# Queuing x sums and weight sums of the first seven-product unit behind the norm's last piece, in each MLP of a two-layer decoder step

## Chip, cores and metric

One core of a Trainium2 chip runs the whole program in one launch. The metric is the device time of one execution in microseconds (us). Engines are named as in the profile: PE is TensorE, DVE is VectorE, ACT is ScalarE, POOL is GpSimd, and SP issues the DMAs.

## What is computed

A step of a two-layer decoder for 512 prompt tokens and 8 x 4 sample tokens, 544 columns in all, with a model width of 1024. Layer 0 mixes tokens with sparse softmax attention, layer 1 with retention; each mixer is followed by an MLP of hidden width 4096. The change lies in the two MLPs:

```python
def _rms(xf):
    return xf * lax.rsqrt(jnp.mean(xf * xf, axis=-1, keepdims=True) + EPS)

def sqrelu_mlp(h, w1, w2):
    return jnp.square(jax.nn.relu(h @ w1)) @ w2
...
        yp = yp + sqrelu_mlp(rms_norm(yp, ln_mlp[i]), mlp_w_in[i], mlp_w_out[i])
        ys = ys + sqrelu_mlp(rms_norm(ys, ln_mlp[i]), mlp_w_in[i], mlp_w_out[i])
```

## The kernel before

**Tiling.** The activations stand transposed in eight tiles `xT[0..7]` of 128 features x 544 tokens; the profile and the queue listings call them x_112 to x_119. Matmuls are done in 32-bit parts: an operand is rounded by ACT (`h`) and DVE takes the rest (`l`), and three products h·h, h·l, l·h go to PE. `split_w` does this for a weight tile (ACT L465 writes `wh`, DVE L466 writes `wl`, two buffers of each), `split_into` for anything else (L662, L663). A 128-column output tile with eight k steps is 48 matmuls of 272 columns, done by `tile_of` (L506) into one of two `mm` PSUM buffers.

**The norm.** The mean square is not applied to x before the matmul but to its result. `take_pair` makes the operands of an x tile as soon as the mixer's output has been added to it (L656), and `square_x` squares it on ACT (L408). The squares of tiles 0 to 5 are added up on POOL, those of tiles 6 and 7 go to PE as they are. `row_rsqrt` sums over the features with small matmuls (L341), and twelve short DVE instructions (L344, then `rsqrt`, L323 to L328) make the root. `spread_rows` spreads it with four small matmuls (L351) and writes `RB`, one half by ACT (L353), one by DVE (L354). Results of a matmul are multiplied by RB as they leave PSUM.

**An MLP.** The first 512 hidden columns are done in four plain tiles, called tile 0 to 3 below. Tile 0 is done before RB exists, so ACT copies it out (`early`, L514); tiles 1 and 2 stay in the two `mm` buffers until DVE takes them with RB (`ev_first`, L1216), and tile 3 needs one of these buffers. ACT then squares (L1209), and `split_into` makes the hidden operands `hs`. The first down unit (two tiles of 24 matmuls, for x_112 and x_113) needs the hidden operands of all four tiles; the next one begins with x_114.

All later hidden columns use seven products in place of eight (`fast_block`, L570 for its matmuls). Such a unit of 256 columns needs sums of its weights: its `split` makes four sums (`add`, L546) and seven splits (`part`, L662 and L663). It also needs sums of x tiles, which `combine` makes once per MLP: two scaled copies on ACT (L444), four DVE instructions (L446, L447, L449, L450) and two splits for each of the four pairs of x tiles. The first such unit, F1 below, stands after the first two down units, the second, F2, two down units later. One product of F1 (`pa`, 12 matmuls) needs no sum of x tiles and only one split.

**What sets the order.** `run` walks over the units; `prepare` asks for loads and splits up to 9 us ahead, and `tick` advances the generators of `combine`. That is only the order of the program: a scheduler then places each instruction on its engine's queue by its own estimate of when it is ready, and allots the buffers. On the chip each queue runs in order, and an instruction whose data is not there holds all behind it. SP's queue waits before a load until a `raw` buffer (four) is free. `late_load` asks for one `raw` tile that nothing writes, before the load of F1.

Of the kernel before, what the change touches and what calls it, by code (L numbers as in the profile page):

```python
# [26 lines left out]
FT = mybir.dt.float32  # L27
# [117 lines left out]
def decoder_step(ctx, tc, x_prompt, x_sample, cache_k, cache_v, cache_kidx, state_ret, page_table,  # L145
# [73 lines left out]


# [98 lines left out]

    def rsqrt(x, w):  # L320

        y, a = w
        V.tensor_scalar(y.bitcast(I32), x.bitcast(I32), 1, None, op0=OP.logical_shift_right)  # L323
        V.tensor_scalar(y.bitcast(I32), y.bitcast(I32), -1.0, 1597463007.0, op0=OP.mult, op1=OP.add)
        for _ in range(3):
            V.tensor_tensor(a, y, y, op=OP.mult)
            V.scalar_tensor_tensor(a, a, -0.5, x, op0=OP.mult, op1=OP.mult)
            V.scalar_tensor_tensor(y, a, 1.5, y, op0=OP.add, op1=OP.mult)  # L328
        return y
# [75 lines left out]
    def square_x(k, n=KT - 2):  # L405

        sq = tmp.tile([128, T], FT, name="sq")
        A.activation(sq, xT[k], AF.Square)  # L408
        if k >= n:
            late.append(sq)  # L410
        elif k == 0:
            G.tensor_copy(acc[:, :T], sq)  # L412
        else:
            G.tensor_tensor(acc[:, :T], sq, acc[:, :T], op=OP.add)

# [3 lines left out]
    def take_pair(k, gi):  # L419
# [17 lines left out]
        square_x(k)  # L437

    def combine(i, gi):

        lo, hi = slice(0, HALF), slice(HALF, T)
        x0, x1 = hs_tile(FT), hs_tile(FT)
        for k, x in ((2 * i, x0), (2 * i + 1, x1)):
            A.activation(x, xT[k], AF.Identity, scale=gains[:, gi * 8 + k:gi * 8 + k + 1])  # L444
        n, t = hs_tile(FT), hs_tile(FT)
        V.tensor_tensor(t[:, lo], x1[:, hi], x0[:, hi], op=OP.subtract)  # L446
        V.tensor_tensor(n[:, lo], x0[:, lo], x0[:, hi], op=OP.subtract)  # L447
# [72 lines left out]
    def fast_block(src, c0, evac):  # L520
# [14 lines left out]
        def split():  # L535
# [3 lines left out]

            def part(name, a):  # L540
                W[name] = [fp.tile([128, 4, 128], FR, name=n, tag=n, bufs=b) for n, b in (("sh", 6), ("sl", 5))]
                split_into(*W[name], a)

            def add(a, b):
                t = fp.tile([128, 4, 128], FT, name="ss", tag="ss", bufs=3)
                V.tensor_tensor(t, a, b, op=OP.add)  # L546
# [655 lines left out]
    def mlp(l, done):  # L1202
        with ExitStack() as st:
# [15 lines left out]
            def up(c):  # L1219
# [9 lines left out]
                return fast_block(mlp_w_in[l], 512 * c, ev) + fast_block(mlp_w_in[l], 512 * c + 256, ev)  # L1229
# [8 lines left out]
            def late_load(load):  # L1238

                skipped = []  # L1240

                def once():
                    if not skipped:
                        skipped.append(raw_tile())
                    return load()
                return once

# [3 lines left out]
            for c in range(n):  # L1251
                down = dense4(mlp_w_out[l], 4 * c, lambda c=c: H[c], add_to_x(done if c == n - 1 else None))
                nxt = up(c + 1) if c + 1 < n else []
                if c == 0:
                    nxt[0].update(before=combined, load=late_load(nxt[0]["load"]))
# [348 lines left out]
```

## Time and profile before

| what | value |
|---|---|
| three runs | 1584.3, 1580.71, 1584.08 us; median 1584.08 |
| profiled execution | 1581.1 us, of which the span from first to last instruction is 1579.2 |
| mean granted TensorE clock | 0.992 of 2.4 GHz |
| DVE, ACT busy | 67% and 39% of the span |
| first MLP, second MLP begin | about 288 and 1190 us |

The span is cut by the profile into rows of one instruction, or of some that follow each other. A row gives its start and its duration. Rows that follow without a gap overlap a little, so the time that an instruction costs its queue is the distance from its start to the next one's start. A bracket at a row's end gives the time for which the engine had nothing to run before it, and what it is taken to have waited for.

### The profile page before, as it was taken

What the parts mean: (1) busy time and instruction counts of PE and PEld (TensorE: products, weight loads), DVE (VectorE), ACT (ScalarE), POOL (GpSimd) and SP (SyncE); (2) the same over time, 40 slices, a digit from 0 to 9 for tenths busy, and PEclk for the clock granted to TensorE, in tenths of its full rate; (3) what the DMA queues carried; (4) which work ended last, traced back from release to release, by engine and by line L of the source; (5) the groups of instructions that cost most, each with busy time, mean ns of one, the idle gap of its engine ahead of it and who ended that gap; (6) DMA issues with size and microseconds to landing.
All of it is one profiled execution on the core that took longest, in us unless ns stands there. A gap on an engine that the chain in (4) does not pass through costs nothing.

```text
span 1579.2 us, 28176 instructions
## 1 busy us (share of the span) xinstructions
PE 1527.9 (97%) x11670; PEld 1440.2 (91%) x11670; DVE 1059.9 (67%) x1950; ACT 611.9 (39%) x1036; POOL 190.5 (12%) x172
## 2 busy tenths in 40 slices
PE   7989899999999999999999999999998999999998
PEld 6689559899999999999899999999988999999998
DVE  6599774778677676556566465565568687677653
ACT  4423663545444444423232232223236454444432
POOL 3220320100000000212221122121210000000000
PEclk9999999999999999999999999999999999999999
DMA  6533252222332233223724622722812322332211
GB/s 177 156 98 94 71 185 81 81 81 81 107 107 86 82 101 107 79 79 109 246 67 163 197 84 91 260 71 73 274 60 64 105 83 82 107 107 82 83 51 57
DMA packets 135774, 172.53 MB, mean 109 GB/s; under 512 B 11660, under 2 KB 92630, under 8 KB 135646
## 3 DMA queue, kind: packets, MB, share of 16 engines
q1 hardware_dynamic: 135578, 170.72, 33.3%
q8 instruction: 91, 1.49, 0.4%
q14 instruction: 37, 0.30, 0.1%
q10 hardware_dynamic: 68, 0.02, 0.0%
HBM read 148.34 MB, written 25.01 MB: 110 GB/s over the span
## 4 chain that ended last, share of the span: by engine, by line
PE 87%; DVE 8%; DMA 2%; ACT 2%; issue 1%; SPq 0%; DVEq 0%; ACTq 0%
PE mm L506 56%; PE mm L570 16%; PE pa L570 2%; PE pb L1487 2%; PE pb L1513 1%; PE pa L1431 1%; DMA raw<-in_mlp_w_in_dram 1%; PE pa L1457 1%; DVE wl L466 1%; PE pb L1468 1%; PE pa L1041 1%; DVE sc L781 1%; PE pa L1014 1%; DVE m L780 1%; PE pb L1100 1%
## 5 line engine op out<-in xcount | busy, mean ns | idle before, releaser
L506 PE MATMUL mm<-xs,wh 128*128 128x272 f32 (+1 forms) x2784 | 501.4, 295 | 13.5 <-ACT r L1209 5.9
L506 PEld LDWEIGHTS mm<-xs,wh 128*128 128x128 f32 (+1 forms) x2784 | 410.0, 190 | 27.5 <-issue 8.9
L506 PE MATMUL mm<-hs,wh 128*128 128x272 f32 x2304 | 393.4, 289 | 3.2 <-DVE x L656 2.0
L506 PEld LDWEIGHTS mm<-hs,wh 128*128 128x128 f32 x2304 | 329.6, 189 | 5.5 <-DVE x L656 2.6
L465 ACT ACTIVATE wh<-raw 128x1024 fp32r<-128x1024 f32 x159 | 167.9, 1057 | 382.0 <-PE mm L506 356.9
L506 PE MATMUL mm<-xs,wl 128*128 128x272 f32 (+1 forms) x1392 | 297.5, 292 | 0.0
L570 PE MATMUL mm<-xs,sh 128*128 128x272 f32 x1344 | 259.1, 289 | 3.1 <-ACT r L583 1.8
L506 PE MATMUL mm<-hs,wl 128*128 128x272 f32 x1152 | 241.1, 288 | 0.0
L656 DVE TENSOR_TENSOR x<-mm,x 128x544 f32<-128x544 f32 x176 | 127.0, 723 | 163.4 <-PE mm L506 162.1
L506 PEld LDWEIGHTS mm<-xs,wl 128*128 128x128 f32 (+1 forms) x1392 | 222.7, 190 | 3.0 <-issue 1.1
L570 PEld LDWEIGHTS mm<-xs,sh 128*128 128x128 f32 x1344 | 210.3, 188 | 5.8 <-ACT r L586 3.5
L466 DVE TENSOR_TENSOR wl<-raw,wh 128x1024 fp32r<-128x1024 f32 x151 | 188.7, 1250 | 16.9 <-ACT wh L465 9.3
L570 PE MATMUL mm<-xs,sl 128*128 128x272 f32 x672 | 192.8, 287 | 0.0
L506 PEld LDWEIGHTS mm<-hs,wl 128*128 128x128 f32 x1152 | 182.1, 188 | 0.2
L570 PEld LDWEIGHTS mm<-xs,sl 128*128 128x128 f32 x672 | 126.3, 188 | 0.0
L662 ACT ACTIVATE sh<-ss 128x512 fp32r<-128x512 f32 x112 | 70.6, 630 | 123.8 <-PE mm L570 118.7
L663 DVE TENSOR_TENSOR sl<-ss,sh 128x512 fp32r<-128x512 f32 x112 | 76.7, 686 | 16.2 <-PE mm L570 16.2
L662 ACT ACTIVATE sh<-raw 128x512 fp32r<-128x512 f32 x84 | 53.1, 632 | 88.2 <-PE mm L570 70.8
L663 DVE TENSOR_TENSOR sl<-raw,sh 128x512 fp32r<-128x512 f32 x84 | 58.6, 698 | 9.3 <-PE mm L570 9.3
L1470 DVE SCALAR_TENSOR_TENSOR raw<-raw,pb 128x512 f32<-128x512 f32 x64 | 43.3, 684 | 24.9 <-PE pb L1468 15.8
L663 DVE TENSOR_TENSOR hs<-r,hs 128x544 fp32r<-128x544 f32 x64 | 46.1, 720 | 16.0 <-ACT hs L662 15.8
L412 POOL COPY acc<-sq 128x544 f32<-128x544 f32 x4 | 3.1, 780 | 444.8 <-ACT sq L408 444.8
(345 smaller groups left out, 1814.6 us busy)
## 6 DMA issues: line engine op xcount, KB each, us to landing
raw<-in_mlp_w_in_dram SPq DMA_DIRECT2D x32, 1024.0 KB
raw<-in_mlp_w_out_dram SPq DMA_DIRECT2D x32, 1024.0 KB
raw<-in_ret_w_in_dram SPq DMA_DIRECT2D x24, 1024.0 KB
raw<-in_state_ret_dram SPq DMA_DIRECT2D x32, 512.0 KB
out_dram<-raw SPq DMA_DIRECT2D x32, 512.0 KB
raw<-in_ret_w_out_dram SPq DMA_DIRECT2D x8, 1024.0 KB
raw<-in_att_w_in_dram SPq DMA_DIRECT2D x7, 1024.0 KB
raw<-in_cache_k_dram SPq DMA_DIRECT2D x32, 128.0 KB
```

Source lines behind the costliest of these rows:

```text
L465: A.activation(h, view, AF.Copy)
L466: eng.tensor_tensor(l, view, h.bitcast(FT), op=OP.subtract)
L506: PE.matmul(ps[:m, c, :HALF], w[:, k, m * t:m * (t + 1)], x[c] if isinstance(x, tuple) else x[:, HALF * c:HALF * (c + 1)], start=(k == 0 a ...
L570: PE.matmul(ps, a[:, i, :], b, start=(first and i == 0 and j == 0), stop=(i == 3 and j == 2), skip_group_check=True)
L656: V.tensor_tensor(two(xT[m]), halves(ps), two(xT[m]), op=OP.add)
L662: A.activation(dst_h, src, AF.Copy)
L663: V.tensor_tensor(dst_l, src, dst_h.bitcast(FT), op=OP.subtract)
L780: V.max(out=m8, in_=sc)
L781: V.match_replace(out=sc, in_to_replace=m8, in_values=sc, imm_value=TAKEN)
L1014: PE.matmul(ps[:, :W], qT[h][:, 128 * blk:128 * (blk + 1)], kT[h // 4][:, :W], start=True, stop=True)
L1470: V.scalar_tensor_tensor(sl, sl, gam4[h], pu, op0=OP.mult, op1=OP.add)
L1487: PE.matmul(ps[:, SP - WJ[j]:], v[:, j, 128 * e:128 * (e + 1)], a[:, AM[j]:AM[j] + WJ[j]], start=(j == 0 and v is vh and a is am[0]), stop ...
```

## The change

`behind(marks)` gives each instruction that is made inside it an order behind the marked instructions on the same engine; no semaphore is added. The marks are `last_in["N"]`, the last DVE instruction of the latest `rsqrt`, and `last_in["A"]`, the latest `square_x` on ACT. Behind them go: in each `combine`, the two scaled copies and the first two differences; and for F1 alone (`first`), all sums and splits of its weights. `late_load` is dropped. No instruction is added or taken away.

```diff
@@ -217,6 +217,14 @@
             for c in calls[1:]:
                 c()
 
+    @contextmanager
+    def behind(marks):
+
+        with ExitStack() as st:
+            for m in marks:
+                st.enter_context(tc.issue_after(m.ins))
+            yield
+
 
     follow, side, held = [], [], []
     norm = {"pending": False}
@@ -317,6 +325,8 @@
         return cr[:rows, lo:hi] if hi <= NCR else ca[:rows, lo - NCR:hi - NCR]
 
 
+    last_in = {}
+
     def rsqrt(x, w):
 
         y, a = w
@@ -325,7 +335,7 @@
         for _ in range(3):
             V.tensor_tensor(a, y, y, op=OP.mult)
             V.scalar_tensor_tensor(a, a, -0.5, x, op0=OP.mult, op1=OP.mult)
-            V.scalar_tensor_tensor(y, a, 1.5, y, op0=OP.add, op1=OP.mult)
+            last_in["N"] = V.scalar_tensor_tensor(y, a, 1.5, y, op0=OP.add, op1=OP.mult)
         return y
 
     def rsqrt_columns(x, n):
@@ -405,13 +415,14 @@
     def square_x(k, n=KT - 2):
 
         sq = tmp.tile([128, T], FT, name="sq")
-        A.activation(sq, xT[k], AF.Square)
+        ins = A.activation(sq, xT[k], AF.Square)
         if k >= n:
             late.append(sq)
         elif k == 0:
             G.tensor_copy(acc[:, :T], sq)
         else:
             G.tensor_tensor(acc[:, :T], sq, acc[:, :T], op=OP.add)
+        return ins
 
     XC = [{} for _ in range(KT // 2)]
     XP = [None] * KT
@@ -434,17 +445,19 @@
             h, l = XP[k] = xs_tile(), xs_tile()
             split(h, l, xT[k])
             XC[k // 2].update(b21=(h[:, lo], l[:, lo]), b22=(h[:, hi], l[:, hi]))
-        square_x(k)
+        last_in["A"] = square_x(k)
 
     def combine(i, gi):
 
         lo, hi = slice(0, HALF), slice(HALF, T)
-        x0, x1 = hs_tile(FT), hs_tile(FT)
-        for k, x in ((2 * i, x0), (2 * i + 1, x1)):
-            A.activation(x, xT[k], AF.Identity, scale=gains[:, gi * 8 + k:gi * 8 + k + 1])
-        n, t = hs_tile(FT), hs_tile(FT)
-        V.tensor_tensor(t[:, lo], x1[:, hi], x0[:, hi], op=OP.subtract)
-        V.tensor_tensor(n[:, lo], x0[:, lo], x0[:, hi], op=OP.subtract)
+        marks = list(last_in.values())
+        with behind(marks):
+            x0, x1 = hs_tile(FT), hs_tile(FT)
+            for k, x in ((2 * i, x0), (2 * i + 1, x1)):
+                A.activation(x, xT[k], AF.Identity, scale=gains[:, gi * 8 + k:gi * 8 + k + 1])
+            n, t = hs_tile(FT), hs_tile(FT)
+            V.tensor_tensor(t[:, lo], x1[:, hi], x0[:, hi], op=OP.subtract)
+            V.tensor_tensor(n[:, lo], x0[:, lo], x0[:, hi], op=OP.subtract)
         yield 0.9
         V.scalar_tensor_tensor(n[:, hi], n[:, lo], -1.0, x1[:, hi], op0=OP.mult, op1=OP.subtract)
         V.scalar_tensor_tensor(t[:, hi], n[:, hi], -1.0, x1[:, lo], op0=OP.mult, op1=OP.subtract)
@@ -517,7 +530,7 @@
                     release()
                 yield 1.5
 
-    def fast_block(src, c0, evac):
+    def fast_block(src, c0, evac, first=False):
 
 
 
@@ -537,13 +550,17 @@
             v = view().rearrange("p (i j) (f c) -> p i j f c", j=2, f=2)
             a11, a21, a12, a22 = (v[:, :, j, f, :] for j in range(2) for f in range(2))
 
+            marks = list(last_in.values()) if first else ()
+
             def part(name, a):
                 W[name] = [fp.tile([128, 4, 128], FR, name=n, tag=n, bufs=b) for n, b in (("sh", 6), ("sl", 5))]
-                split_into(*W[name], a)
+                with behind(marks):
+                    split_into(*W[name], a)
 
             def add(a, b):
                 t = fp.tile([128, 4, 128], FT, name="ss", tag="ss", bufs=3)
-                V.tensor_tensor(t, a, b, op=OP.add)
+                with behind(marks):
+                    V.tensor_tensor(t, a, b, op=OP.add)
                 return t
             part("a11", a11)
             yield 1.5
@@ -1226,7 +1243,8 @@
                     else:
                         V.scalar_tensor_tensor(r, r, 0.0, RB, op0=OP.max, op1=OP.mult)
                     hidden(c, r)
-                return fast_block(mlp_w_in[l], 512 * c, ev) + fast_block(mlp_w_in[l], 512 * c + 256, ev)
+                return fast_block(mlp_w_in[l], 512 * c, ev, c == 1) + \
+                    fast_block(mlp_w_in[l], 512 * c + 256, ev)
 
             n = DFF // 512
             H[0] = []
@@ -1234,16 +1252,6 @@
                 block(mlp_w_in[l], 0, 8, 256, 256, XP, ev_first)
             gens = [combine(i, 2 + l) for i in range(KT // 2)]
             side.append([gens, 0.7, 0.0])
-
-            def late_load(load):
-
-                skipped = []
-
-                def once():
-                    if not skipped:
-                        skipped.append(raw_tile())
-                    return load()
-                return once
 
             def combined():
                 drain(gens)
@@ -1252,7 +1260,7 @@
                 down = dense4(mlp_w_out[l], 4 * c, lambda c=c: H[c], add_to_x(done if c == n - 1 else None))
                 nxt = up(c + 1) if c + 1 < n else []
                 if c == 0:
-                    nxt[0].update(before=combined, load=late_load(nxt[0]["load"]))
+                    nxt[0]["before"] = combined
                     units += down[:2] + nxt[:1] + down[2:] + nxt[1:]
                 else:
                     units += nxt[:1] + down[:2] + nxt[1:] + down[2:]
```

Line numbers in the listings below are those of the file that each comes from: L656, L466, L426, L546, L663, L354, L344, L328 and L1216 of the kernel before are L673, L479, L437, L563, L680, L364, L354, L338 and L1233 of the changed one. SP's and POOL's queues hold the same rows in the same order in both.

DVE, first MLP, where the last x tiles arrive (`x_118<-mm` adds the mixer's output to x_118; `ss` are sums of F1's weights, `sl` are rests of its splits). Before:

```order
L426 SCALAR_TENSOR_TENSOR xs<-x_117,gains,xs 128x544
L656 TENSOR_TENSOR x_118<-mm,x_118 128x544
L663 TENSOR_TENSOR sl<-ss,sh 128x512 x2
L663 TENSOR_TENSOR sl<-raw,sh 128x512
L656 TENSOR_TENSOR x_119<-mm,x_119 128x544
L663 TENSOR_TENSOR sl<-ss,sh 128x512
L546 TENSOR_TENSOR ss<-ss,raw 128x512
L466 TENSOR_TENSOR wl<-raw,wh 128x1024
L426 SCALAR_TENSOR_TENSOR xs<-x_118,gains,xs 128x272
L426 SCALAR_TENSOR_TENSOR hs<-x_118,gains,hs 128x272
L446 TENSOR_TENSOR hs<-hs 128x272
L447 TENSOR_TENSOR hs<-hs 128x272
```

The change:

```order
L437 SCALAR_TENSOR_TENSOR xs<-x_117,gains,xs 128x544
L673 TENSOR_TENSOR x_118<-mm,x_118 128x544
L437 SCALAR_TENSOR_TENSOR xs<-x_118,gains,xs 128x272
L437 SCALAR_TENSOR_TENSOR hs<-x_118,gains,hs 128x272
L673 TENSOR_TENSOR x_119<-mm,x_119 128x544
L479 TENSOR_TENSOR wl<-raw,wh 128x1024
L437 SCALAR_TENSOR_TENSOR xs<-x_119,gains,xs 128x544
L354 TENSOR_SCALAR rw<-pb 128x136
```

F1's sums and splits and the x sums no longer stand among the x tiles; the norm's first instruction (`rw<-pb`) follows the last x tile's operand at once.

DVE, second MLP, from the end of the root to the first results that RB releases (`rw<-rw` is the root's last instruction, `RB<-pb` the DVE half of RB). Before, where `ss<-raw` are sums of F2's weights:

```order
L328 SCALAR_TENSOR_TENSOR rw<-rw 128x136
L546 TENSOR_TENSOR ss<-raw 128x512 x2
L466 TENSOR_TENSOR wl<-raw,wh 128x1024
L354 COPY RB<-pb 128x272
L663 TENSOR_TENSOR sl<-ss,sh 128x512
L1216 SCALAR_TENSOR_TENSOR r<-early,RB 128x544
L1216 SCALAR_TENSOR_TENSOR r<-mm,RB 128x544 x2
```

The change, where `ss` up to RB are sums of F1's weights:

```order
L338 SCALAR_TENSOR_TENSOR rw<-rw 128x136
L459 TENSOR_TENSOR hs<-hs 128x272
L460 TENSOR_TENSOR hs<-hs 128x272
L680 TENSOR_TENSOR sl<-raw,sh 128x512
L563 TENSOR_TENSOR ss<-raw 128x512 x2
L462 SCALAR_TENSOR_TENSOR hs<-hs 128x272
L563 TENSOR_TENSOR ss<-ss,raw 128x512
L463 SCALAR_TENSOR_TENSOR hs<-hs 128x272
L479 TENSOR_TENSOR wl<-raw,wh 128x1024
L364 COPY RB<-pb 128x272
```

Four instructions of the first `combine`, a split and three sums of F1 now stand between the root and RB; F2's two sums have left that place.

DVE, second MLP, the rows that follow at once in the changed kernel:

```order
L680 TENSOR_TENSOR sl<-ss,sh 128x512 x2
L680 TENSOR_TENSOR sl<-raw,sh 128x512
L1233 SCALAR_TENSOR_TENSOR r<-early,RB 128x544
L1233 SCALAR_TENSOR_TENSOR r<-mm,RB 128x544
L680 TENSOR_TENSOR sl<-ss,sh 128x512
L680 TENSOR_TENSOR xs<-hs,xs 128x544
L563 TENSOR_TENSOR ss<-ss,raw 128x512
L680 TENSOR_TENSOR xs<-hs,xs 128x544
L1233 SCALAR_TENSOR_TENSOR r<-mm,RB 128x544
L563 TENSOR_TENSOR ss<-raw 128x512
```

F1's other splits stand before and among the three results that RB releases, and F2's first sum (the last row) stands behind all three. On both MLPs the changed listing reads the same from RB to here.

## Rows read from the trace of the kernel before

**Rows 1.** the page, parts 1 and 2: span; busy time, share of the span and instructions

```profile
span 1579.2 us, 28176 instructions
...
PE 1527.9 (97%) x11670; PEld 1440.2 (91%) x11670; DVE 1059.9 (67%) x1950; ACT 611.9 (39%) x1036; POOL 190.5 (12%) x172
```

**Rows 2.** timeline of PE, first MLP: start us, us, instruction [idle before <-releaser]

```profile
283.77 0.66 PE L506 MATMUL mm<-hs,wh 128*128 128x272 f32 x4
...
288.04 0.42 PE L506 MATMUL mm<-hs,wl 128*128 128x272 f32 x2
...
290.38 0.37 PE L506 MATMUL mm<-xs,wh 128*128 128x272 f32 x1 [1.56 <-DVE x L656]
...
314.17 0.39 PE L506 MATMUL mm<-xs,wh 128*128 128x272 f32 x1 [1.88 <-ACT r L1209]
...
330.45 0.77 PE L506 MATMUL mm<-hs,wh 128*128 128x272 f32 x4 [1.33 <-DVE x L656]
```

**Rows 3.** timeline of PE, second MLP

```profile
1189.39 0.41 PE L506 MATMUL mm<-xs,wl 128*128 128x272 f32 x2
...
1190.97 0.36 PE L506 MATMUL mm<-xs,wh 128*128 128x272 f32 x1 [0.80 <-DVE x L656]
...
1216.86 0.56 PE L506 MATMUL mm<-xs,wh 128*128 128x272 f32 x1 [4.04 <-ACT r L1209]
...
1232.70 0.78 PE L506 MATMUL mm<-hs,wh 128*128 128x272 f32 x4 [0.31 <-DVE x L656]
```

**Rows 4.** chain of waits in order of time, both MLPs: start us, us, what

```profile
295.80 0.37 PE pb L341 x8
...
303.68 1.07 ACT wh L465
...
314.17 7.79 PE mm L506 x48
...
1206.57 5.47 DMA raw<-in_mlp_w_in_dram
...
1216.86 8.72 PE mm L506 x48
```

**Rows 5.** stretches: length, busy by engine (instructions), PEclk, DMA share, GB/s

```profile
315.00:320.00 5.00, 5.00 (x32) 5.00 (x31) 4.96 (x10) 4.47 (x8) 0.00 (x0) 0.72 0.00 0
...
325.00:330.00 5.00, 3.37 (x24) 2.85 (x22) 5.00 (x11) 3.46 (x7) 0.00 (x0) 1.00 0.69 210
...
1215.00:1220.00 5.00, 3.15 (x14) 3.18 (x15) 3.86 (x7) 3.89 (x7) 0.00 (x0) 0.55 0.00 0
```

**Rows 6.** timeline of DVE, first MLP

```profile
299.14 0.30 DVE L344 TENSOR_SCALAR rw<-pb 128x136 f32<-128x136 f32 x1 [1.08 <-PE pb L341]
...
314.57 1.22 DVE L466 TENSOR_TENSOR wl<-raw,wh 128x1024 fp32r<-128x1024 f32 x1
...
315.70 0.69 DVE L663 TENSOR_TENSOR sl<-ss,sh 128x512 fp32r<-128x512 f32 x1
...
316.30 0.72 DVE L663 TENSOR_TENSOR hs<-r,hs 128x544 fp32r<-128x544 f32 x1
...
316.94 0.69 DVE L546 TENSOR_TENSOR ss<-ss,raw 128x512 f32<-128x512 f32 x1
...
317.54 0.44 DVE L446 TENSOR_TENSOR hs<-hs 128x272 f32<-128x272 f32 x1
...
317.89 0.44 DVE L447 TENSOR_TENSOR hs<-hs 128x272 f32<-128x272 f32 x1
```

**Rows 7.** timeline of DVE, second MLP

```profile
1202.52 0.30 DVE L327 SCALAR_TENSOR_TENSOR rw<-rw 128x136 f32<-128x136 f32 x1
...
1202.85 0.30 DVE L328 SCALAR_TENSOR_TENSOR rw<-rw 128x136 f32<-128x136 f32 x1
...
1212.06 1.29 DVE L546 TENSOR_TENSOR ss<-raw 128x512 f32<-128x512 f32 x2 [4.31 <-DMA raw<-in_mlp_w_in_dram]
...
1214.41 0.43 DVE L354 COPY RB<-pb 128x272 f32<-128x272 f32 x1
```

## Prediction

> **What bounds the kernel now.** Read first the page's busy shares: PE is busy for 1527.9 of 1579.2 us [rows 1], so nothing but PE's own gaps, or matmuls at a lower clock, can be won. Next, the timeline of PE, for the brackets at the two places where an MLP begins. Each stretch is counted from t0, the end of the matmuls of the last x tile (x_119): 288.04 + 0.42 = 288.46 in the first MLP [rows 2], 1189.39 + 0.41 = 1189.80 in the second [rows 3]. It ends where the second down unit starts (x_114): 330.45 and 1232.70, the last rows of these groups. So the stretch takes 42.0 us in the first MLP and 42.9 in the second.
>
> At full clock 34 matmuls lie between the starts 283.77 and 288.04 [rows 2]: 0.1256 us each, 6.0 for a tile of 48. Against this, four things are lost per stretch:
> - the wait before tile 0, 1.56 and 0.80 [rows 2, 3]; DVE had not yet emptied the x tiles' PSUM, since sums and splits of F1 stood before `x_118<-mm` and `x_119<-mm` in its queue;
> - the wait before tile 3, 1.88 and 4.04. The page names ACT, but tile 3 needs an `mm` buffer that DVE frees with L1216. In the second MLP DVE stood 4.31 us for F2's weights to land (`ss<-raw`, 1212.06), with RB behind it (1214.41) [rows 7];
> - tile 3 itself, 7.79 and 8.72 [rows 4] instead of 6.0: 1.8 and 2.7. The granted clock was 0.72 and 0.55 in the stretches there [rows 5], so part of it ran at the 1.2 GHz level, after PE had stood still;
> - the first down unit: from tile 3's end (314.17 + 7.79 = 321.96; 1216.86 + 8.72 = 1225.58) to x_114, 8.5 and 7.1 instead of 6.0: 2.5 and 1.1, waits for the last hidden operands.
>
> Together 7.7 and 8.7 us; the rest, 34.3 and 34.2, is PE's work.
>
> **The change, part by part.** Dropping `late_load` removes no instruction, and SP's rows stand as before: nothing. The rest moves work behind the norm, per MLP and on DVE: four sums and five splits of F1, four instructions and two splits of the first `combine`.
>
> *Before t0.* The DVE listing shows the x tiles free of F1's work. The evacuation of x_119 then starts at t0, and tile 0 finds its buffer (that of x_118) and its operands: the first wait goes.
>
> *The norm.* The sums of x_119's square now stand behind 32 matmuls (4.0 us) and three groups of four small ones (0.37 a group [rows 4]) with gaps: the root starts at about t0 + 5.5, against 299.14 = t0 + 10.7 before [rows 6]. Its square is ready earlier, at some t0 + 2.2: evacuation, a rounding, the operand and the square on ACT.
>
> *DVE from there to RB.* A short instruction of the root costs 0.33 (1202.52 to 1202.85 [rows 7]). From the distances of starts [rows 6]: a `wl` 1.13, a 512-wide sum or split 0.60, a 544-wide instruction 0.64, a 272-wide one 0.35. Eight of the root: t0 + 8.1. Then `wl` of tile 2, whose rounding on ACT (1.07 [rows 4]) waits for tile 0's end at t0 + 7.3: done at t0 + 9.4. Four more of the root: + 10.7. Then the new part: four x instructions, a split and three sums, 4 x 0.35 + 4 x 0.60 = 3.8: + 14.5. `wl` of tile 3 (rounding behind tile 1's end, t0 + 13.3): + 15.6. RB: + 16.0, against 1214.41 = t0 + 24.6 in the second MLP before. So 3.8 us are put ahead of RB, and it still comes earlier, since the root starts 5.2 earlier and no load is waited for.
>
> *Tile 3.* Three splits (1.8) and two results (1.28) more, and the buffer is free at t0 + 19.1. PE gets there, by its own rows without the waits, at 314.17 - 1.88 - 1.56 - 288.46 = t0 + 22.3. It waits for nothing, with 3.2 us to spare; so I take the clock as staying up, and tile 3 ends at t0 + 28.3.
>
> *The first down unit.* It needs tile 3's hidden operand, and DVE is now the later one. From RB to there its queue holds nine 512-wide instructions, ten of 544, eleven of 272 and two `wl`: 5.4 + 6.4 + 3.9 + 2.3 = 18.0, and the last rest stands at t0 + 34.0. One of 272, two of 544 and the evacuation of x_112 (0.35 + 1.28 + 0.72) later x_114 starts: **t0 + 36.3**. PE loses 2.0 us here, 36.3 - 28.3 - 6.0.
>
> *F2's load* is issued when `wl` of tile 3 is done (t0 + 15.6), takes 5.47 [rows 4], and lands at t0 + 21.1. Its first sum is reached at t0 + 22.1 and stands behind the results that RB releases: covered, by 1.0 us.
>
> *ACT* has as much to do as before; the last rounding of `hs` waits for nothing later than DVE does, by the same sums.
>
> **The sum.** 42.0 - 36.3 = 5.7 and 42.9 - 36.3 = 6.6. By the losses: 1.56 + 1.88 + 1.8 + 0.5 and 0.80 + 4.04 + 2.7 - 0.9. After x_114 both programs have the same work in nearly the same order, with PE as the bound, so the **12.3 us** stay won. The profiled execution took 1581.1: 1568.8. The shown runs lie between 1580.71 and 1584.3, and their median, 1584.08, is 3.0 above the profiled one; I take the middle of the runs, 1582.5, and forecast **1570.2**.
>
> Bounds. If DVE never held PE, the stretch would be PE's work alone, 34.3: 7.7 + 8.6 = 16.3 us won, 1566.2. If DVE's instructions cost their full durations (0.69, 0.72, 0.44, 1.22 [rows 6]) and not the distance of starts, the 32 behind RB take 2.8 us longer in each MLP: 12.3 - 5.6 = 6.7 won, 1575.8. I take the distances, since DVE ran through its rows at 314.57 to 317.89 at this pace.
>
> **A rule against it.** PE stood still for 1.88 us and 4.04 us before the lower clock appeared, while after the waits in the first down unit, which come to 2.5 us in pieces, the stretch 325 to 330 shows 1.00 [rows 5]. In the changed kernel the 2.0 us come in such pieces, so my sum has no lower clock. The Trainium skill (TensorE: Matmul & The Clock Gate, section "A second HAM failure mode: psum-queue depth-cycling") says otherwise of short pauses: between groups of matmuls that go round the PSUM buffers they can by themselves make the clock go down and up. By that rule the lower clock would come back, at the down unit; the row at 325 speaks against it, for pauses of this size.
>
> **Rivals.**
> 1. *The clock falls at the first down unit.* PE arrives there earlier and waits for DVE; if the pauses join into one, the matmuls behind run at the lower level for as long as tile 3 did: 1.8 + 2.7 = 4.5 us given back, 1574.7. For it: the fall after 1.88 us; against it: the row at 325.
> 2. *DVE's pile costs more than its rows.* ACT's queue holds roundings of weights that wait for PE ahead of the hidden operands, and DVE waits for ACT; the price is that of full durations: 1575.8.
> 3. *All is given back.* If the root starts no earlier than before, because PE or ACT is late with the squares, the chain from the root shifts by 5.2: x_114 at t0 + 41.5, about as before: 1582. Against it: nothing stands before x_119 on DVE any more.
> 4. *Slower: F2's load lands late.* The load is issued only after `wl` of tile 3, and that stands behind 3.8 us of new work; the first sum of F2 holds DVE's queue, and all the hidden operands behind it. The point from which this costs more than is won is a load of 5.47 + 1.0 + 5.7 = 12.2 us. At three times the row's 5.47, 16.4, DVE stands for 9.9 us and x_114 starts at t0 + 46.2: 4.2 and 3.3 us lost, 1590.0. For it: DVE did stand 4.31 us for this load [rows 7]; against it: it took 5.47, and no other load is due with it.
>
> **Chances.** Forecast 0.66, rival 1 0.12, rival 2 0.12, rival 3 0.06, rival 4 0.04. The 0.3% that a measurement of this kernel can tell is 4.7 us, a limit of 1577.8 below the middle of the runs: forecast, rivals 1 and 2 are faster (0.90, I say 0.89), rival 3 is no change (0.06, with the upper edge of rival 2: 0.07), rival 4 slower (0.04). The range takes in the forecast, its bounds and rivals 1 and 2, and 3 us below and 2 above for the scatter of the runs shown: 1563 to 1578.
>
> **What would show it.** Right: no bracket on PE before tile 0 and tile 3; `RB<-pb` near t0 + 16; a clock of 1.00 across tile 3; `ss<-raw` without a wait for a load; x_114 at t0 + 36. Wrong: a long bracket in the first down unit with a lower clock behind it (rival 1), x_114 after t0 + 38 at full clock (rival 2), the root at t0 + 10 (rival 3), DVE waiting at F2's first sum (rival 4). A gain or loss outside these two stretches would show that the sum looked at the wrong place.

## The result, and the profile after

The changed kernel takes **1568.29 us** (median of five runs, 1567.75 to 1572.91) against 1584.3 for the kernel before on the same chip (1580.71 to 1587.15): a ratio of 0.9916, with a 95% interval of 0.9898 to 0.9933, so 13.3 us less (10.6 to 16.2; the two medians alone lie 16.0 apart). Forecast were 1570.2, a gain of 12.3, and 1563 to 1578. The profiled execution took 1572.79. The page, part 1:

```profile
span 1570.7 us, 28174 instructions
...
PE 1528.9 (97%) x11670; PEld 1439.9 (92%) x11670; DVE 1057.1 (67%) x1950; ACT 611.2 (39%) x1036; POOL 191.0 (12%) x172
```

PE is as busy as before [rows 1]; what went is its waiting. (Each engine counts the same instructions as before; the two that are fewer in the first line are not among them.) The timeline of PE in the first MLP, then in the second (start, duration, instruction, in brackets the wait before it and its releaser):

```profile
290.75 0.41 PE L519 MATMUL mm<-hs,wl 128*128 128x272 f32 x2
...
291.45 0.40 PE L519 MATMUL mm<-xs,wh 128*128 128x272 f32 x1
...
313.45 0.28 PE L519 MATMUL mm<-xs,wh 128*128 128x272 f32 x1
...
324.74 0.76 PE L519 MATMUL mm<-hs,wh 128*128 128x272 f32 x4 [0.36 <-ACT hs L679]
...
325.68 0.52 PE L519 MATMUL mm<-hs,wh 128*128 128x272 f32 x2 [0.18 <-DVE hs L680]
...
327.94 0.77 PE L519 MATMUL mm<-hs,wh 128*128 128x272 f32 x4 [0.99 <-DVE x L673]
```

```profile
1187.61 0.41 PE L519 MATMUL mm<-xs,wl 128*128 128x272 f32 x2
...
1188.32 0.39 PE L519 MATMUL mm<-xs,wh 128*128 128x272 f32 x1
...
1210.22 0.28 PE L519 MATMUL mm<-xs,wh 128*128 128x272 f32 x1
...
1224.76 0.76 PE L519 MATMUL mm<-hs,wh 128*128 128x272 f32 x4 [0.99 <-DVE x L673]
```

t0 is 290.75 + 0.41 = 291.16. The brackets before tile 0 (291.45) and tile 3 [rows 2] are gone; tile 3 starts at 313.45 = t0 + 22.3, and x_114 at 327.94 = t0 + 36.78 (before: 42.0). The second MLP reads the same: t0 = 1187.61 + 0.41, x_114 at 1224.76 = t0 + 36.74 (before 42.9 [rows 3]). Tile 3 had run in part at the lower clock [rows 5]. The stretches in which it runs now, and between them the one behind x_114 in the first MLP (last columns: granted clock, DMA share, GB/s):

```profile
315.00:320.00 5.00, 5.00 (x42) 5.00 (x41) 5.00 (x10) 4.36 (x8) 0.00 (x0) 1.00 0.01 2
...
330.00:335.00 5.00, 5.00 (x42) 5.00 (x41) 3.55 (x6) 1.00 (x1) 0.00 (x0) 1.00 0.00 0
...
1210.00:1215.00 5.00, 5.00 (x42) 5.00 (x42) 5.00 (x10) 5.00 (x10) 0.00 (x0) 1.00 0.00 0
```

Full clock in all three, and in tile 3's two DVE is busy in 5.00 of 5.00 us. DVE's timeline in the first MLP, the rows that answer to [rows 6, 7]:

```profile
297.03 0.30 DVE L354 TENSOR_SCALAR rw<-pb 128x136 f32<-128x136 f32 x1 [3.07 <-PE pb L351]
...
307.29 0.43 DVE L364 COPY RB<-pb 128x272 f32<-128x272 f32 x1
...
310.08 0.71 DVE L1233 SCALAR_TENSOR_TENSOR r<-mm,RB 128x544 f32<-128x544 f32 x1
...
313.82 0.68 DVE L563 TENSOR_TENSOR ss<-raw 128x512 f32<-128x512 f32 x1
...
324.90 0.72 DVE L680 TENSOR_TENSOR hs<-r,hs 128x544 fp32r<-128x544 f32 x1
...
327.17 0.72 DVE L673 TENSOR_TENSOR x<-mm,x 128x544 f32<-128x544 f32 x1
```

Root at t0 + 5.87, RB at t0 + 16.13, F2's sum at 313.82 without a wait for its load. The chain of waits says what the end of the stretch hangs on:

```profile
313.62 0.77 PE mm L519 x6
...
314.42 1.22 DVE wl L479
...
324.99 0.64 DVE hs L680
...
327.17 0.73 DVE x L673
...
327.94 2.14 PE mm L519 x15
```

From 314.42 to 327.90 the chain runs through DVE alone, one instruction behind the other, up to the evacuation of x_112.

Where the time came from: the two stretches give 41.99 - 36.78 = 5.21 and 42.90 - 36.74 = 6.16, 11.4 us. Below each MLP is also taken to its end: from t0 to the next norm's `RB<-pb` in the first, from t0 to the span's end in the second. The two together are 394.46 + 389.40 = 783.9 before and 388.76 + 382.68 = 771.4 after, 12.4 less. Of this 11.4 lies before x_114. The other 1.0 has no place of its own: PE's matmuls behind x_114, the same in the same order, run ahead evenly, by 0.1 us after 300 of them and by 0.5 after 2700, in each MLP. The profiled execution gained only 8.5 of span, since it came 2.7 us later to the first t0 (291.16 for 288.46) and took 1.2 more between the MLPs (508.1 for 506.9), parts that the change doesn't touch (last section).

### The profile page after: what moved, and what is told of

Same layout as the page of the kernel before. It is cut to its first block, busy times and chain, and to the rows that moved or that the text cites. A ratio compares the mean times of both kernels' runs of the same rounds, so it can differ in the third digit from the quotient of the medians.

```text
span 1570.7 us, 28174 instructions
## 1 busy us (share of the span) xinstructions
PE 1528.9 (97%) x11670; PEld 1439.9 (92%) x11670; DVE 1057.1 (67%) x1950; ACT 611.2 (39%) x1036; POOL 191.0 (12%) x172
## 4 chain that ended last, share of the span: by engine, by line
PE 89%; DVE 7%; DMA 2%; ACT 1%; issue 1%; SPq 0%; DVEq 0%; ACTq 0%
PE mm L519 58%; PE mm L587 16%; PE pa L587 2%; PE pb L1495 2%; PE pb L1521 1%; PE pa L1439 1%; PE pa L1465 1%; PE pb L1476 1%; PE pa L1058 1%; PE pa L1031 1%; DVE wl L479 1%; PE pa L1384 0%; DVE m L797 0%; DVE sl L680 0%; DMA out_dram<-raw 0%
## 5 line engine op out<-in xcount | busy, mean ns | idle before, releaser
L673 DVE TENSOR_TENSOR x<-mm,x 128x544 f32<-128x544 f32 x176 | 127.2, 724 | 161.7 <-PE mm L519 160.5
L479 DVE TENSOR_TENSOR wl<-raw,wh 128x1024 fp32r<-128x1024 f32 x151 | 188.7, 1251 | 18.3 <-ACT wh L478 10.4
L680 DVE TENSOR_TENSOR sl<-ss,sh 128x512 fp32r<-128x512 f32 x112 | 76.7, 686 | 16.2 <-PE mm L587 16.2
L680 DVE TENSOR_TENSOR sl<-raw,sh 128x512 fp32r<-128x512 f32 x84 | 57.5, 684 | 9.3 <-PE mm L587 9.3
L680 DVE TENSOR_TENSOR hs<-r,hs 128x544 fp32r<-128x544 f32 x64 | 46.1, 720 | 16.0 <-ACT hs L679 15.8
```

The source lines that it names most:

```text
L479: eng.tensor_tensor(l, view, h.bitcast(FT), op=OP.subtract)
L673: V.tensor_tensor(two(xT[m]), halves(ps), two(xT[m]), op=OP.add)
L680: V.tensor_tensor(dst_l, src, dst_h.bitcast(FT), op=OP.subtract)
```

## The experiments

All in one table, from one profile each: start of the root, of RB's copy and of x_114 behind t0, in the first / second MLP; the two MLPs to their ends, less the 783.9 of before; and the ratio of the timed runs to those of the kernel before beside them, with its interval. The copy and the root are the rows `RB<-pb` and the first `rw<-pb` of DVE's timeline. The column of the MLPs is one execution each, the ratio is of several, and they don't always agree: a1 keeps 5.9 by its profile and 2.7 us by its runs, a2 3.9 and 7.9.

| kernel | root | RB | x_114 | MLPs, us | ratio |
|---|---|---|---|---|---|
| before | 10.7 / 10.5 | 21.9 / 24.6 | 42.0 / 42.9 | 0 | 1 |
| changed | 5.9 / 5.8 | 16.1 / 16.1 | 36.8 / 36.7 | -12.4 | 0.9916 |
| a1 | 8.6 / 9.1 | 18.7 / 18.3 | 39.9 / 38.0 | -5.9 | 0.9983 [0.9965, 1.0001] |
| a2 | 6.7 / 7.4 | 16.6 / 16.6 | 38.0 / 38.0 | -3.9 | 0.9950 [0.9927, 0.9974] |
| a3 | 10.6 / 10.5 | 21.8 / 22.6 | 40.4 / 41.7 | +2.0 | 1.0013 [1.0001, 1.0025] |
| a4 | 5.9 / 5.8 | 16.1 / 16.1 | 37.4 / 37.2 | +7.0 | 1.0037 [1.0023, 1.0050] |
| b1 | 5.9 / 5.8 | 16.1 / 16.1 | 36.8 / 36.7 | -12.5 | 0.9918 [0.9897, 0.9938] |
| b2 | 6.8 / 8.3 | 23.5 / 23.4 | 44.1 / 41.3 | +0.3 | 1.0003 [0.9988, 1.0018] |
| b3 | 6.8 / 8.2 | 22.0 / 21.9 | 41.2 / 41.1 | +0.9 | 1.0017 [1.0003, 1.0032] |
| b4 | 5.9 / 5.7 | 22.0 / 21.8 | 43.8 / 43.6 | +3.6 | one run, 1583.2 |
| c1 | 5.9 / 6.0 | 17.0 / 17.0 | 37.4 / 37.4 | -6.3 | 0.9952 [0.9937, 0.9967] |
| c2 | 6.2 / 6.8 | 17.0 / 17.5 | 37.0 / 37.6 | -11.2 | 0.9941 [0.9920, 0.9961] |
| c3 | 5.9 / 6.1 | 17.0 / 17.0 | 35.4 / 35.5 | -14.4 | 0.9916 [0.9903, 0.9930] |
| d1 | 5.9 / 5.7 | 16.1 / 15.9 | 35.4 / 35.2 | -14.7 | 0.9907 [0.9892, 0.9922] |

**a1: the x sums alone.** The changed kernel with

```diff
-            marks = list(last_in.values()) if first else ()
+            marks = ()
```

> Only the x sums of combine stand behind the norm; F1's weight sums and splits are free again and stand among the x tiles as before. Theory A (the prediction's sum: four separate losses): the wait before tile 0 stays (1.56 and 0.80), the wait before tile 3 and its lower clock go, so the stretch from t0 to x_114 takes 42.0 - 1.88 - 1.8 = 38.3 and 42.9 - 4.04 - 2.7 = 36.2, or less, and 10 us are won. Theory B (RB's copy sets the end: DVE's pile behind it is what x_114 waits for): the root starts about 1 us earlier than before, RB at t0 + 18 to 19, the pile is 3.6 us shorter than in the changed kernel (six instructions of F1 at 0.60 stand ahead of it), x_114 at t0 + 36 to 37. Theory C (only F1's work among the x tiles cost time): the stretch stays at 42.0 and 42.9.

Measured: half of the gain by the profile; by the timed runs 2.7 us, with an interval that takes in no gain at all. None of the three theories had it. The timeline of PE, first MLP:

```profile
295.30 0.37 PE L519 MATMUL mm<-xs,wh 128*128 128x272 f32 x1 [1.64 <-DVE x L673]
...
330.62 0.52 PE L519 MATMUL mm<-hs,wh 128*128 128x272 f32 x2 [2.41 <-DVE hs L680]
...
333.13 1.28 PE L519 MATMUL mm<-hs,wh 128*128 128x272 f32 x4 [1.23 <-DVE x L673]
```

The wait before tile 0 stayed and that before tile 3 went, as theory A had it; but x_114 came 1.6 and 1.8 later than A's sum, because PE met new waits in the first down unit, for DVE. RB at t0 + 18.7 was theory B's, but x_114 follows it by 21.1 and 19.7 us, where the changed kernel has 20.6, not by 3.6 less: in the first MLP a wait of 2.56 for F2's load had come into the pile.

**a2: the weight sums alone.** In `combine`, `marks = []`.

> Only F1's weight sums and splits stand behind the norm; the first pair of x sums and its two splits are free and stand between x_119's evacuation and the root. Theory A: the wait before tile 0 goes, tile 3 waits for nothing, x_114 at t0 + 36 to 37, 11 to 12 us won. Theory B: root at t0 + 6 to 7.5, RB at t0 + 16 to 17, x_114 at t0 + 36 to 37.5. Rival (the x sums carry the gain, because ACT's copies for them stand ahead of the last square): root at t0 + 8 or later, x_114 at t0 + 39 or later, 7 us won or less.

Measured: RB as early as in the changed kernel (+0.5), but x_114 1.2 later, behind waits of 1.28 and 1.34 in the first down unit, and after them the granted clock was 0.53 (330 to 335). So x_114 to the end took 2.9 to 3.1 us more than in the changed kernel, and 12.4 shrank to 3.9. But the profiled execution, 1583.03, is the slowest of six, which go down to 1569.62; the ratio of them all, 0.9950, keeps 7.9 us. Whether the clock falls in every execution isn't shown. By the profiles the two halves, 5.9 and 3.9, don't add up to the whole; by the ratios, 2.7 and 7.9 against 13.3, that can't be said, and the weight sums look the larger half, though the two intervals touch.

**a3: the sums of F2 alone.** The kernel before with `behind`, and for the second unit of the first pair (`second`):

```diff
+                ev_in["V"] = V.scalar_tensor_tensor(two(r), halves(ps), 0.0, two(RB), op0=OP.max, op1=OP.mult)
...
+            marks = list(ev_in.values()) if second else ()
...
+                with behind(marks):
+                    V.tensor_tensor(t, a, b, op=OP.add)
```

> The kernel before, with one thing moved: the sums of the SECOND seven-product unit (F2) stand behind the last result of the first MLP block, so that no load is waited for ahead of RB and of the results that free a buffer. F1 and the x sums stay where they were before. Theory A: first waits stay, the wait before tile 3 shrinks to under 0.5 in both MLPs and its clock is 1.00: 42.0 - 1.88 - 1.8 = 38.3 and 42.9 - 4.04 - 2.7 = 36.2, 10 us won. Theory B (x_114 follows RB's copy): RB does not move in the first MLP (310.33, it waited for PE), so the first MLP wins only the 0.68 that the sum waited for its load, and up to 1.3 of the sums themselves: 40 to 41.3; in the second MLP RB comes at t0 + 19 to 20 and x_114 at t0 + 37 to 38.5; 6 us won. Theory C (F1's work among the x tiles): under 1 us won.

Measured: no gain, 2 us lost. PE, first MLP:

```profile
312.87 0.36 PE L517 MATMUL mm<-xs,wh 128*128 128x272 f32 x1
...
326.86 0.52 PE L517 MATMUL mm<-hs,wh 128*128 128x272 f32 x2 [1.79 <-DVE hs L677]
...
329.47 1.28 PE L517 MATMUL mm<-hs,wh 128*128 128x272 f32 x4 [1.33 <-DVE x L670]
```

Tile 3 no longer waits and runs at full clock, but of the 1.88 + 1.8 that it had cost x_114 comes only 1.6 earlier: the rest stands in the down unit instead, and behind x_114 the granted clock was 0.51 (330 to 335), which gave back more than was won. Theory A falls here: the wait before tile 3 was a symptom. RB had not moved in the first MLP, and x_114 stayed near, as theory B said. In the second MLP theory B missed: RB came at t0 + 22.6 and not at 19 to 20, since a `wl` stands ahead of it that waited 3.52 for its rounding (b3 has more on this), x_114 at 41.7 and not at 37 to 38.5, and tile 3 still waited 2.15. That the clock would fall was in neither.

**a4: F2's sums later still, in the changed kernel**: `hid_in["V"] = split_into(hh, hl, r)`, and `marks = list(hid_in.values())` for the second unit. This was meant to put them behind the rest of tile 3's hidden operand, and does more. The list is read when F2's split begins; by then F1's second result is the latest, and F2's splits stand behind it as well as its sums.

> The changed kernel, and F2's sums behind the last rest of tile 3's hidden operand besides; three sums of 0.60 leave DVE's pile between RB and x_114. Theory B (DVE bounds the first down unit): x_114 at t0 + 35.0 in both MLPs instead of 36.8 and 36.7, 3.5 us faster than the changed kernel. Rival (PE, or ACT's roundings, bound it): x_114 stays at t0 + 36.5 or later. If F2 itself comes too late, PE waits behind x_114, in its products, and the gain is given back there.

Measured: slower than before the change. DVE, then PE:

```profile
321.09 0.72 DVE L680 TENSOR_TENSOR hs<-r,hs 128x544 fp32r<-128x544 f32 x1
...
322.08 1.99 DVE L680 TENSOR_TENSOR xs<-hs,xs 128x544 fp32r<-128x544 f32 x3
...
324.34 1.35 DVE L673 TENSOR_TENSOR x<-mm,x 128x544 f32<-128x544 f32 x2
...
358.09 0.72 DVE L680 TENSOR_TENSOR hs<-r,hs 128x544 fp32r<-128x544 f32 x1 [1.41 <-ACT hs L679]
358.74 0.68 DVE L680 TENSOR_TENSOR sl<-raw,sh 128x512 fp32r<-128x512 f32 x1
359.34 1.29 DVE L563 TENSOR_TENSOR ss<-raw 128x512 f32<-128x512 f32 x2
```

```profile
325.11 0.77 PE L519 MATMUL mm<-hs,wh 128*128 128x272 f32 x4 [1.97 <-DVE x L673]
...
359.48 0.39 PE L587 MATMUL mm<-xs,sl 128*128 128x272 f32 x1 [4.22 <-DVE sl L680]
```

The three sums left the pile, and the order was filled from behind: three splits of x sums (1.99) now stand ahead of x_112's evacuation. And F2's weights come too late: its first split and sums (358.74, 359.34) follow the rest of F1's second hidden operand (358.09) and not tile 3's (321.09), and PE waits 4.22 for them in the first MLP and 4.21 in the second. Behind that wait the granted clock was 0.50 in the first MLP (360 to 365). Compared with the changed kernel 9.9 and 8.4 us are lost behind x_114 in all. So a4 shows the refilling of the pile; what F2's sums right behind tile 3's operand would do wasn't run.

**b1: `late_load` put back** into the changed kernel.

> The changed kernel with late_load put back; every engine's queue is that of the changed kernel. All theories: no difference, 1568 to 1573, x_114 at t0 + 36.8 and 36.7. It shows how far two builds with the same queues lie apart on one chip, and it stands beside the next two as the changed kernel's own time.

Measured: 1570.08, 36.8 and 36.7. Dropping it does nothing; and two profiles with the same queues agree to 0.1 us from t0 on.

**b2: behind the last operand instead of the root.** In the changed kernel the mark on the root is replaced:

```diff
-            last_in["N"] = V.scalar_tensor_tensor(y, a, 1.5, y, op0=OP.add, op1=OP.mult)
+            V.scalar_tensor_tensor(y, a, 1.5, y, op0=OP.add, op1=OP.mult)
...
-            V.scalar_tensor_tensor(l, x, g, h.bitcast(FT), op0=OP.mult, op1=OP.subtract)
+            last_in["X"] = V.scalar_tensor_tensor(l, x, g, h.bitcast(FT), op0=OP.mult, op1=OP.subtract)
```

> The same work is queued behind the rest of the last x tile's operand on DVE and the last square on ACT, instead of behind the root: the 3.07 us in which DVE waits for the sums of squares ahead of the root are filled with F1's sums and the first x sums. Theory D (all of DVE's work from x_119 to x_112's evacuation is one chain, and its length sets x_114): root at t0 + 6 to 7.5, x_114 2 to 2.4 us earlier than in the changed kernel, t0 + 34.4 to 35, where PE's own work (34.3) is the bound; 4 us faster than the changed kernel in all. Theory E (x_114 follows the root's start, about 31 us behind it in all kernels so far): every us by which the root is later costs one, x_114 at t0 + 37 to 38.5, 1 to 4 us slower than the changed kernel. F2's first sums stand ahead of RB again; if its load is waited for there, the wait shows at that row.

Measured: all the gain gone, though the x tiles stay free of F1's work and PE doesn't wait before tile 0. Both theories fall: x_114 comes 37.3 and 33.0 us behind the root, not 31. DVE, first MLP:

```profile
297.12 0.29 DVE L354 TENSOR_SCALAR rw<-pb 128x136 f32<-128x136 f32 x1
...
305.26 1.23 DVE L479 TENSOR_TENSOR wl<-raw,wh 128x1024 fp32r<-128x1024 f32 x1 [1.52 <-ACT wh L478]
...
312.09 0.69 DVE L563 TENSOR_TENSOR ss<-raw 128x512 f32<-128x512 f32 x1 [3.72 <-DMA raw<-in_mlp_w_in_dram]
...
313.84 0.43 DVE L364 COPY RB<-pb 128x272 f32<-128x272 f32 x1
```

In the first MLP the root starts only 0.9 later than in the changed kernel, but F1's work stands among its instructions. So six of the twelve fall behind a `wl`, whose rounding on ACT waits for the end of a tile on PE; and F2's load is waited for ahead of RB. RB comes 7.4 later.

**b3: b2 with F2's sums, and here its splits too, behind the last result**, as in a3.

> As b2, and the sums of the second unit behind the last result of the first MLP block, so that no load is waited for ahead of RB. Theory D: x_114 at t0 + 34.4 to 35. Theory E: t0 + 37 to 38.5. If b2 shows a wait for the load and b3 doesn't, their difference is its price. If F2's weights come too late, PE waits in F2's products, and the time behind x_114 grows.

Measured: the load is waited for no more, and RB gains 1.4 to 1.5. It still comes 5.9 later than in the changed kernel, behind a `wl` again; ACT's timeline has why:

```profile
304.61 1.06 ACT L478 ACTIVATE wh<-raw 128x1024 fp32r<-128x1024 f32 x1 [2.92 <-PE mm L519]
...
310.59 1.06 ACT L478 ACTIVATE wh<-raw 128x1024 fp32r<-128x1024 f32 x1 [4.92 <-PE mm L519]
```

The roundings stand 6.0 apart, the length of a tile: a root that misses one waits for the next.

**b4: a longer root**, all else as in the changed kernel:

```diff
+        for _ in range(repeat[0]):
+            V.tensor_scalar(w[:, 0], ps[:, :QT], 1.0 / n, EPS, op0=OP.mult, op1=OP.add)
```

> The changed kernel with the first instruction of the root written 15 times instead of once in both MLPs: 14 x 0.33 = 4.6 us more on DVE between the sums of squares and the root's result, while the x tiles stay free of F1's work and tile 0 doesn't wait. Theory D or E (one chain on DVE): x_114 at t0 + 41 to 41.5, nearly all the gain gone, 9 us slower than the changed kernel (1578 to 1583). Rival (separate losses): tile 0 still doesn't wait, tile 3 waits 1 to 2 us, x_114 at t0 + 38 or earlier.

Measured: 1583.2, x_114 at t0 + 43.8 and 43.6, later than either side had it. The first MLP (t0 at 287.39), DVE's copy and PE:

```profile
309.42 0.43 DVE L365 COPY RB<-pb 128x272 f32<-128x272 f32 x1
```

```profile
311.69 0.58 PE L588 MATMUL pa<-xs,sh 128*128 128x272 f32 x1 [3.36 <-ACT sh L680]
...
331.15 0.77 PE L520 MATMUL mm<-hs,wh 128*128 128x272 f32 x4 [1.59 <-DVE x L674]
```

This separates the root from the order among the x tiles: F1's work, the x sums and F2's sums stay behind the root, tile 0 doesn't wait, and 4.6 us more of root bring RB to t0 + 22.0 and take all of the gain back. It is not RB alone that moves, but all that stands behind the root on DVE. RB comes 5.9 later and x_114 7.0, more than the 4.6, since a third `wl` now stands ahead of RB, and the rest of the order changed too. PE waits 3.36 for a split of F1's weights and 0.33 more for tile 3's buffer, and the lower clock (0.77 in 1205 to 1220) returns.

**c1: F1's first sums in the gap ahead of the root.** Their mark is the rest of the last x operand, that of the splits stays:

```diff
-                with behind(marks):
+                with behind(list(last_op.values()) if first else ()):
                     V.tensor_tensor(t, a, b, op=OP.add)
```

> The changed kernel, but F1's first three sums (which need no rounding on ACT) may stand right behind the rest of x_119's operand; its splits and the x sums stay behind the root. They fill 1.8 of the 3.07 us in which DVE waits ahead of the root, and PE's queue is that of the changed kernel. Theory F (what counts is that the root's twelve instructions run unbroken, so that RB's copy comes early; work in the gap ahead of the root is free): root at t0 + 5.9, RB at t0 + 15.5 to 16.1, the last hidden operand's rest 0.5 to 1.8 earlier, x_114 at t0 + 35.5 to 36.8. Theory E (anything ahead of the root delays it, as in b2): root at t0 + 6.5 or later, RB at t0 + 18 or later, x_114 at t0 + 38 or later.

Measured: the root is on time, so work in the gap is free, but RB comes 0.8 to 0.9 later and x_114 0.6, in neither theory's range for RB: again other work was drawn forward, five splits of F1 ahead of RB, where the changed kernel has one, and four splits of x sums just ahead of x_112's evacuation, where the changed kernel has two. PE and the granted clock, second MLP:

```profile
1221.83 0.52 PE L519 MATMUL mm<-hs,wh 128*128 128x272 f32 x2 [1.39 <-DVE hs L680]
...
1224.43 1.27 PE L519 MATMUL mm<-hs,wh 128*128 128x272 f32 x4 [1.34 <-DVE x L673]
```

```profile
1225.00:1230.00 5.00, 5.00 (x24) 5.00 (x23) 2.41 (x4) 0.03 (x1) 0.00 (x0) 0.50 0.00 0
```

After the two waits PE ran at the 1.2 GHz level, and from x_114 to the end this MLP took 349.1 us for 345.9: 0.6 us of pile became 3.8.

**c2: the mark on DVE alone**, `last_in["A"] = square_x(k)` back to `square_x(k)`.

> Only the mark on DVE's root holds the work back; the mark on ACT's last square is dropped, so ACT's copies for the x sums and its roundings of F1's weights may stand ahead of that square. DVE's queue up to the root is that of the changed kernel but for one wl. If the mark on DVE carries the change: root at t0 + 5.9 to 6.5, RB at t0 + 16 to 17, x_114 at t0 + 36.5 to 37.5, 10 us faster than before. If ACT's order matters: the last square is late by the copies ahead of it (two of 0.75 and a rounding, 2 us), the root at t0 + 8, RB at t0 + 18 or later, x_114 at t0 + 38 or later.

Measured: 11.2 of 12.4 us by the profile, 0.9941 against 0.9916 by the runs, with intervals that overlap. The mark on VectorE carries most of the change; the one on ScalarE is worth 0.3 to 1.0 of the root's start.

**c3 and d1: the x sums of the last of the four pairs behind tile 3's hidden operand**, c3 on c1, d1 on the changed kernel:

```diff
+        while i == 3 and len(first_hidden()) < 4:
+            yield 0.8
-        marks = list(last_in.values())
+        marks = list(last_in.values()) + (list(hid_in.values()) if i == 3 else [])
```

> As c1, and the x sums of the last of the four pairs stand behind tile 3's hidden operand; PE's queue is that of the changed kernel. Between RB and that operand's rest DVE has 14.2 us of work instead of 18.0. Theory F: RB at t0 + 15.5 to 16.1, the rest done by t0 + 31, no wait of PE in the first down unit, x_114 at t0 + 34.3 to 34.8, which is PE's own work; 4 to 5 us faster than the changed kernel, 1564 to 1568. If F1's operands then come too late, PE waits at F1 and the time behind x_114 grows by what is won.

> The changed kernel with one thing more: the x sums of the last of the four pairs stand behind tile 3's hidden operand, F1's sums stay behind the root. Up to RB the queues are those of the changed kernel: root at t0 + 5.9, RB at t0 + 16.1. Theory F (RB and what DVE does between it and x_112 set x_114): three 272-wide instructions (1.05) leave the row ahead of the last rest, one split less stands ahead of x_112, x_114 at t0 + 35.0 to 35.6 in both MLPs, 2.3 to 3.5 us faster than the changed kernel in the two stretches together, no lower clock. Rival (DVE's queue is refilled from behind, as in a4 and c1): x_114 at t0 + 36.5 or later. If F1's operands come too late, PE waits in F1's products and the time from x_114 to the MLP's end grows.

Measured: x_114 at t0 + 35.4 and 35.5 in c3, a microsecond later than its theory F had it, and 35.4 and 35.2 in d1, as forecast. PE's only wait in d1's two stretches, first and second MLP:

```profile
322.83 0.77 PE L526 MATMUL mm<-hs,wh 128*128 128x272 f32 x4 [0.69 <-DVE x L680]
...
1218.06 0.78 PE L526 MATMUL mm<-hs,wh 128*128 128x272 f32 x4 [0.78 <-DVE x L680]
```

This is what RB and the pile behind it predict: RB is left alone (16.1), three instructions leave the pile, and PE has no new wait behind x_114. (Of the 2.9 won at x_114 2.2 are left at the MLPs' ends; the rest goes evenly over them, as the 1.0 of the changed kernel came.) c3 has its RB 0.9 later and so wins no more for the sums in the gap. By the profile d1 is the best version, 2.2 us below the changed kernel in the MLPs; by the timed runs (0.9907 and 0.9916, with overlapping intervals) it can't be told from it.

## Why the prediction was right

*The steps.* Root forecast at t0 + 5.5, measured 5.9; the end of RB's copy 16.0, measured 16.5 (its start, which the table has, 16.1); PE at tile 3 at 22.3, measured 22.3, and no wait; clock 1.00; F2's sum without a wait; last hidden operand 34.0, measured 325.62 - 291.16 = 34.5; x_114 36.3, measured 36.8 and 36.7. The only term off is the root, 0.4 late, and it is carried through to the end: the gaps around the small matmuls ahead of it cost more than was put in. Of the 12.3 us forecast for the two stretches 11.4 were won there, and 1.0 more behind x_114, where the forecast had put nothing and the change isn't shown to be the cause. That 12.3 and 12.4 agree so closely is luck; the 5.2 and 6.2 against 5.7 and 6.6 are the measure of the sum. Distances of starts were the right price for DVE's rows, so rival 2 falls: from the end of RB's copy to the end of the last rest DVE took 34.5 - 16.5 = 18.0 us, as summed.

*What was right for less than its reason.* The prediction also reads the gain as four losses that go: 1.56 + 1.88 + 1.8 + 0.5. The sum closes, but they are not four causes. In a3's first MLP the wait before tile 3 and its lower clock go (in the second the wait halves), in b2 and b3 the wait before tile 0 goes, and nothing is won. What they have in common is RB: over the 28 stretches of the table x_114 starts 18.0 to 21.9 us behind RB's copy, wherever RB stands between 15.9 and 24.6. The spread of 3.9 lies in the pile. b4 shows that a longer root, with nothing else asked for, takes the gain back, and d1 that a shorter pile alone, with RB where it was, brings x_114 forward. The chain that the prediction worked out, root, RB, pile, was the cause; the list of losses was its shadow on PE. RB itself wasn't moved without the rest of DVE's queue in any run.

*Rival 3* (the chain from the root shifts by 5.2, x_114 at t0 + 41.5, about as before) is near what b4 built: 43.7 and a time as before. (Its price is 1580.6 by its own numbers, 1582.5 - 0.5 - 1.4, and not 1582.) *Rival 4* (F2's load late): the wait came back in b2, 3.72, and a1, 2.56; in the changed kernel the margin held.

*Rival 1 and the rule on the clock.* In the changed kernel the waits in the first down unit, 0.36 + 0.18 + 0.99, were followed by a clock of 1.00, as forecast. But the prediction took one row of before as evidence for all pauses of this size, and that was too sure. That row, 325 to 330, even ends inside the second of its two waits (0.75, then 1.33 up to 330.45 [rows 2]); the stretch behind it, 330 to 335, shows 1.00 too. In other kernels, after 1.39 and 1.34 (c1), 1.28 and 1.34 (a2) or 1.79 and 1.33 (a3) the lower level came, while after 1.69 and 0.98 (a1, second MLP) it did not. In a4 nearly the same waits had both outcomes: after 0.49 and 1.97 in the first MLP the clock fell to 0.50, after 0.49 and 1.98 in the second it stayed at 1.00. So the rule of the Trainium skill (TensorE: Matmul & The Clock Gate, section "A second HAM failure mode: psum-queue depth-cycling"), by which short pauses between groups of matmuls can make the clock go down and up, fits c1, a2 and a3. How far the changed kernel lies from such a fall isn't shown, and what decides is left open: the length of the waits alone does not.

## What to carry to other kernels

A norm's short serial chain should run as unbroken as it can on its engine, with everything else behind it: one rounding that waits for a tile, among or behind its instructions, can delay its result by the length of that tile (5.9 of 6.0 us in b3). Waits that PE shows one after another can be one delay seen several times; find the row that moves them all, and test it by lengthening it alone. Taking work out of a full queue wins little if the order is filled from behind: hold back what would move up, and look at the unit that needs the held work. And see in the trace what a mark came to stand on: the list of a4 was read later than meant.

## What the runs showed of the hardware that was not expected

Two executions with the same queues don't reach the first MLP at the same time. The stretch from 40 to 80 us, in attention, of the changed kernel and of b1:

```profile
40.00:80.00 40.00, 38.80 (x258) 28.30 (x262) 20.27 (x50) 14.09 (x31) 8.12 (x4) 0.87 0.48 149
```

```profile
40.00:80.00 40.00, 38.02 (x282) 27.28 (x281) 24.40 (x63) 15.93 (x35) 8.49 (x4) 1.00 0.51 159
```

At a granted clock of 0.87 the stretch holds 258 matmuls, at 1.00 it holds 282 (281 in the kernel before, at 1.00); t0 comes at 291.16 and at 288.84. Over all profiles t0 lies between 285.86 and 293.28, further apart than half of the gain: single runs of this kernel say little, stretches counted from t0 say much.

In the kernel before, one split of F1 took 1.84 us where the same instruction takes 0.68 a few rows on; POOL had an addition at the time (timelines of DVE and of POOL):

```profile
286.46 1.84 DVE L663 TENSOR_TENSOR sl<-raw,sh 128x512 fp32r<-128x512 f32 x1
...
291.36 0.68 DVE L663 TENSOR_TENSOR sl<-raw,sh 128x512 fp32r<-128x512 f32 x1
```

```profile
286.08 1.68 POOL L414 TENSOR_TENSOR acc<-sq,acc 128x544 f32<-128x544 f32 x1 [2.87 <-ACT sq L408]
```

POOL's addition ends at 287.76 and the split at 288.30, about half a microsecond later, as if it had only begun then. By the Trainium skill (SBUF — State Buffer, section "SBUF: two separate sides") the two engines share a pair of ports, and an instruction of DVE with two SBUF inputs is blocked while one of POOL that reads SBUF holds it; the rows agree. It is a further reason to keep work between SBUF tiles out of the rows among the x tiles, where the squares are summed on POOL. No run here measures it by itself.
